# Layer 0's modulation vectors: from 128-column stationary blocks of w_mod to a 2-column stationary silu(c), with other planner settings

## The chip, the cores and the metric

The kernel runs on one core of a Trainium2 chip. The metric is the device time of one launch in microseconds (us). Before the change it is 2589.57 us, the median of three runs (2583.79, 2589.57 and 2592.41).

## The reference, cut to what matters

The reference is a two-layer backbone over 1024 latent tokens and 256 context tokens of width 1024, all in float32. Each layer normalises the tokens, scales and shifts them with modulation vectors, projects them by one large matrix, runs three branches (Fourier mixing F, differential attention A, a bidirectional state-space scan S), merges the branches by gates, and adds the result to the stream. The change touches the first lines of layer 0:

```
mod_l = jax.nn.silu(c) @ w_mod[l] + b_mod[l]          # (1, 1024) @ (1024, 3072)
mod_c = jax.nn.silu(c_ctx) @ w_mod[l] + b_mod[l]
sh_l, sc_l, g_l = jnp.split(mod_l[:, None, :], 3, axis=-1)
h_l = rmsnorm(x, norm_w[l]) * (1.0 + sc_l) + sh_l      # the same for the context with mod_c
... = jnp.split(h_l @ w_in[l], split_at, axis=-1)
```

Shift (part 0) and scale (part 1) for both vectors c and c_ctx are needed before anything can be projected. That is two products of a 2 x 1024 matrix with a 1024 x 1024 one, whose weights are 8 MB.

## The kernel before, in words

**Engines and planner.** TensorE (PE) does matrix products and transposes, VectorE (DVE) and ScalarE (ACT) the elementwise work, GpSimd (POOL) a few copies, and SyncE (SP) issues every transfer. The program is not in written order. Python generators ("threads") emit operations: `m` (the three branches), `p` (start and projections), `f` (normalisation of the later rows, merge, finish), `e` (gates of the last branch), `g` (layer 1's modulation and both gate vectors); weight loading and splitting is tagged `w`. While the program is built, a list scheduler (class Scheduler) keeps a modelled clock for each engine, and each time places the ready operation of the best priority. The priority is the number of the operation in order of emission less `BIAS[thread]`. A thread may have at most `AHEAD[thread]` emitted operations that are not yet placed. So the order on each engine is fixed at build time, and another cost or setting anywhere can redraw the order of the whole program. Nearly all instructions are issued by one line, L400 (`o.fn(...)`), so profile rows are told apart by their tiles.

**Storage.** There are 28 slots of 128 x 1288 floats (tile `ar`) for everything large, and eight PSUM banks (tile `ps`). A bank is given out when its first matmul is placed.

**Layer 0's start** (`start`, `mod0`). Ten slots are reserved for the tokens. `mod0` goes over k = 0..7 (row blocks of w_mod) and, in each, over part 1 and part 0: it loads one 128 x 1024 tile (512 KB), and for each of its eight 128-column blocks it issues one float32 matmul with the block stationary and `cs[:, k]` (128 x 2: silu of c and of c_ctx) moving. All 128 matmuls accumulate into one bank t (128 x 32), which a matmul with a zeroed operand clears. The result stands with channels on partitions, as the next step wants it. Between the tiles the loop issues other loads: the constants with k = 1, layer 0's parameters with k = 3, the first four token tiles with k = X_AT (4), and the first projection weight (`fu01`, two raw tiles) with k = W_AT (7). Then modT is formed from bank t, `mod_finish` makes the scale and shift `ab`, and `norm_T` transposes the normalised tokens and applies `ab`. The first projection (`proj_fu`) comes after that. The remaining six token tiles are loaded once `mod0` has been emitted.

**The rest.** All large products are float16 pairs (high and low part, three products each). In layer 1 the branches run in the order F, A, S. S goes through its chunks one after the other (`ssd_scan`), then come the last merge and the output.

Of the kernel before, what the change touches and what calls it, by code (L numbers as in the profile page):

```python
# [14 lines left out]
AF = mybir.ActivationFunctionType  # L15
# [28 lines left out]
NSLOT = 28  # L44
NW = 8
RAW = 2
BIAS = {'m': 1200, 'p': 300, 'w': 1000, 'f': 0, 'e': -50000, 'g': -100000}
AHEAD = {'m': 120, 'p': 120, 'f': 40, 'e': 27, 'g': 6}
MAXB = {'m': 4, 'p': 3, 'f': 3, 'e': 1, 'w': 1, 'g': 1}
LEAST = (1, 1)  # L50
WLIM = {'p': 2, 'f': 4, 'e': 1}
# [2 lines left out]
RES = 2  # L54
BOR, BMAX = 2, 4
HOLD = 0.25
X_AT, W_AT = 4, 7
G_AFTER = 'fu2'
F_START, F_FIN = 1000, 300
C_FIN = (2, 2)  # L60
# [90 lines left out]
class Scheduler:  # L151
# [3 lines left out]
    def __init__(self, nc):  # L155
# [11 lines left out]
        self.fixed = []  # L167
        self.bias = dict(BIAS)
        self.slot_of = {}
# [248 lines left out]
class Builder:  # L418
# [316 lines left out]
    def mod0(self, L):  # L735

        nc, V = self.nc, self.nc.vector
        t = self.mm(True)
        nc.bias['w'] = 0
        zero = self.small(32)  # L740
        nc.gpsimd.memset(zero, 0.0)
        for k in range(8):
            for part in (1, 0):
                yield ('slots', 1)
                s = self.alloc()
                nc.sync.dma_start(s.v(1024), self.A['wm'][0, part, k])
                if k == 0 and part:
                    self.mul(t[:, 0:32], s.v(1024)[:, 0:128], zero, True, False)
                for b in range(8):
                    c = 16 * part + 2 * b  # L750
                    self.mul(t[:, c:c + 2], s.v(1024)[:, b * 128:b * 128 + 128], self.cs[:, k], False, k == 7 and not part and b == 7)
                s.drop()
            if k == 1:
                self.consts()
            if k == 3:
                self.params(0)
            if k == X_AT:
                self.load_x(0)
            if k == W_AT:
                self.fetch_p = True  # L760
                self.prefetch()
        modT = self.cst.tile([128, 16, 2], F32, name="modT0")
        V.tensor_tensor(modT, t[:, :32].rearrange("p (b s) -> p b s", s=2), self.pv[0][:, 0:16].unsqueeze(2).to_broadcast([128, 16, 2]), ALU.add)
        nc.close('p', True)
        self.mod_finish(L, modT)
        nc.bias['w'] = BIAS['w']
        yield
# [107 lines left out]
    def start_rest(self, L):  # L875
        yield ('need', (0, 'h0'))
        self.nc.bias['f'] = F_START
        for i in (1, 2):
            self.norm_scale(self.groups[i], self.x[i])
            yield from self.norm_T(L, self.groups[i], self.x[i])  # L880
        self.nc.bias['f'] = BIAS['f']

# [797 lines left out]
    def finish(self, L, N):  # L1680
# [76 lines left out]
        if l == 0:  # L1757
            yield from steps
        self.ahead['f'] = AHEAD['f']
        self.ev.add((l + 1, 'fin'))  # L1760
# [144 lines left out]
    def build(self, layers=2):  # L1905
        self.setup()
        self.layers, self.later = layers, 0
        self.ahead = dict(AHEAD)
        Ls = []
# [179 lines left out]
```

## Time and profile before

| | |
|---|---|
| median of three runs | 2589.57 us |
| the profiled execution's own time | 2585.78 us |
| its span, first to last instruction | 2584.0 us |
| TensorE busy in the span | 2486.6 us (96%) |
| VectorE, ScalarE busy | 1821.3 us (70%), 1268.0 us (49%) |
| mean granted TensorE clock | 0.983 |
| all 16 DMA engines' share of the span | 34.5% |

A float32 matmul or transpose in the program is two MATMUL records in the trace, so that the 128 products of `mod0` are 256 records. A matmul's record is longer than the distance to the next one, since matmuls are pipelined: the rate is read from many records in a row. A group's "busy" counts overlapping records once.

### The profile page before, as it was taken

To read this page: it belongs to the slowest core of one execution; us is meant where nothing else is said; L and a number is where in the kernel's file an instruction comes from. 1 tells how busy PE (TensorE), PEld (TensorE's weight loads), DVE (VectorE), ACT (ScalarE), POOL (GpSimd) and SP (SyncE) were. 2 spreads that over 40 slices of the span, in tenths; PEclk is the share of its full clock that TensorE was granted. 3 is DMA by queue.
4 is the path that set the end of the run, shared out by engine and by line. 5 is a ranking of instruction groups with operands and counts; after the bars stand their busy time and mean duration, and the time that the engine had idled before them with its cause. 6 is when DMAs were issued, how large, how long until landed. Compare 5 with 4: busy or idle time off the path is not lost. (4 is left out here: it accounts for less than half of the span.)

```text
span 2584.0 us, 42400 instructions
## 1 busy us (share of the span) xinstructions
PE 2486.6 (96%) x16800; PEld 1572.5 (61%) x16800; DVE 1821.3 (70%) x3823; ACT 1268.0 (49%) x2398; POOL 47.5 (2%) x93
## 2 busy tenths in 40 slices
PE   9999999999999999999999999999999999998698
PEld 9655665657565665575587556555655556556467
DVE  1868565687877898468956775776477768748766
ACT  2654453545655564456513654554464656446221
POOL 0200000000000000000000000000000000000000
PEclk9999999999999999999999999999999999999699
DMA  6132243354433334213722122434343423232331
GB/s 250 50 131 77 65 101 82 80 148 111 112 78 89 131 116 142 87 55 119 286 79 99 57 90 66 109 94 98 82 122 88 100 95 106 78 102 87 131 131 66
DMA packets 256979, 270.61 MB, mean 105 GB/s; under 512 B 181062, under 2 KB 191110, under 8 KB 256780
## 3 DMA queue, kind: packets, MB, share of 16 engines
q1 hardware_dynamic: 256780, 267.89, 34.5%
q8 instruction: 132, 2.16, 0.3%
q14 instruction: 67, 0.55, 0.1%
HBM read 178.02 MB, written 36.88 MB: 83 GB/s over the span
## 5 line engine op out<-in xcount | busy, mean ns | idle before, releaser
L400 PE MATMUL ps<-ar,w 128*128 128x512 f16 (+1 forms) x7296 | 1476.8, 355 | 3.7 <-ACT w L400 2.7
L400 PEld LDWEIGHTS <-w 128*128 128x128 f16 x7296 | 708.7, 98 | 649.6 <-issue 17.0
L400 PEld LDWEIGHTS <-ar 128*128 128x128 f16 x8000 | 648.9, 98 | 231.3 <-issue 26.4
L400 PE MATMUL ps<-ar,ar 128*128 128x128 f16 (+4 forms) x4564 | 564.7, 274 | 31.2 <-DVE ar L400 18.4
L400 PE MATMUL ps<-w,ar 128*128 128x256 f16 x3312 | 396.0, 273 | 0.0
L400 ACT ACTIVATE ar<-ps,s1m,qksc 128x1280 f32<-128x1280 f32 (+1 forms) x144 | 190.1, 1320 | 194.4 <-DVE s1m L400 158.0
L400 DVE TENSOR_REDUCE s1m<-ps 128x1 f32<-128x1280 f32 (+1 forms) x144 | 196.9, 1368 | 101.8 <-PE ps L400 91.0
L400 ACT ACTIVATE w<-raw 128x1024 f16<-128x1024 f32 x147 | 154.5, 1051 | 180.9 <-PE ps L400 105.5
L400 ACT ACTIVATE ar<-ar 128x1280 f16<-128x1280 f32 (+5 forms) x140 | 138.1, 987 | 104.6 <-DVE ar L400 103.0
L400 DVE TENSOR_TENSOR ar<-ar,ar 128x1280 f16<-128x1280 f32 (+3 forms) x116 | 123.4, 1064 | 9.3 <-ACT ar L400 9.0
L400 DVE SCALAR_TENSOR_TENSOR ar<-ar,pv,ar 128x1284 f32<-128x1284 f32 (+1 forms) x64 | 97.1, 1517 | 32.9 <-ACT ar L400 32.3
L400 ACT ACTIVATE ar<-ps 128x128 f32<-128x128 f32 (+5 forms) x192 | 67.3, 386 | 104.6 <-PE ps L400 103.6
L400 ACT ACTIVATE ar<-ps,ds 128x512 f32<-128x512 f32 (+1 forms) x86 | 53.9, 627 | 114.4 <-PE ps L400 114.3
L400 DVE SCALAR_TENSOR_TENSOR ar<-ar,s1m,ar 128x1280 f32<-128x1280 f32 (+1 forms) x72 | 103.1, 1432 | 0.0
L400 ACT ACTIVATE ar<-ar,ar 128x128 f32<-128x128 f32 x288 | 90.1, 388 | 22.8 <-DMA ar<-rows 21.7
L400 ACT ACTIVATE w<-raw,s1p 128x1024 f16<-128x1024 f32 x72 | 79.0, 1138 | 33.9 <-DVE s1p L400 33.7
L400 DVE SCALAR_TENSOR_TENSOR w<-raw,s1p,w 128x1024 f16<-128x1024 f32 x72 | 89.8, 1279 | 7.9 <-ACT w L400 7.7
L400 PE MATMUL ps<-k,ar 128*128 128x128 f32 (+1 forms) x492 | 79.3, 289 | 15.5 <-DVE ar L400 14.7
L400 DVE SCALAR_TENSOR_TENSOR w<-raw,s1f,w 128x1024 f16<-128x1024 f32 x65 | 81.4, 1279 | 9.8 <-ACT w L400 9.8
L400 PEld LDWEIGHTS ps<-k,ar 128*128 128x128 f32 x492 | 63.1, 157 | 38.2 <-DVE ar L400 23.3
L400 DVE SCALAR_TENSOR_TENSOR scrf<-ps,ds,ar 128x256 f32<-128x256 f32 x72 | 34.7, 482 | 72.6 <-PE ps L400 72.3
L400 PEld LDWEIGHTS ps<-ar,ar 128*128 128x128 f32 x428 | 67.0, 206 | 29.7 <-DVE ar L400 20.8
(218 smaller groups left out, 2157.0 us busy)
## 6 DMA issues: line engine op xcount, KB each, us to landing
raw<-in_wt SPq DMA_DIRECT2D x160, 512.0 KB, 4.7
ar<-in_wm SPq DMA_DIRECT2D x48, 512.0 KB, 6.4
ar<-rows SPq DMA_DIRECT2D x36, 512.0 KB, 4.5
yp<-scrf SPq DMA_DIRECT2D x64, 256.0 KB, 2.2
ar<-in_x SPq DMA_DIRECT2D x20, 512.0 KB, 9.5
gs<-scre SPq DMA_DIRECT2D x32, 256.0 KB, 2.0
scrf<-yp SPq DMA_DIRECT2D x32, 256.0 KB, 2.7
ar<-ar SPq DMA_DIRECT2D x32, 160.0 KB, 2.8
```

What stands on the lines that cost most here:

```text
L400: o.fn(*(place(a) for a in o.args), **{k: place(a) for k, a in o.kw.items()})
```

## The change

`mod0` makes silu(c) the stationary operand (128 x 2) and streams the w_mod tile in two halves of 512 columns. Each part has two banks of 2 x 512, so that 32 matmuls replace the 128. The results stand with channels along the free dimension on two partitions. For each part ScalarE copies one half and VectorE the other into a row slot (two more slots), and 16 TensorE transposes of 2 x 128 bring the channels back onto partitions, into a bank t as before. The zeroed operand, its memset and its matmul are gone. Beside that, six planner settings change: the biases of m, p and w, the lookahead of m and f, and X_AT.

```diff
-BIAS = {'m': 1200, 'p': 300, 'w': 1000, 'f': 0, 'e': -50000, 'g': -100000}
-AHEAD = {'m': 120, 'p': 120, 'f': 40, 'e': 27, 'g': 6}
+BIAS = {'m': 1000, 'p': 200, 'w': 400, 'f': 0, 'e': -50000, 'g': -100000}
+AHEAD = {'m': 80, 'p': 120, 'f': 30, 'e': 27, 'g': 6}
-X_AT, W_AT = 4, 7
+X_AT, W_AT = 3, 7
     def mod0(self, L):
-        t = self.mm(True)
+        row = [self.alloc(), self.alloc()]
+        p = [[self.mm(True), self.mm(True)] for _ in range(2)]
         nc.bias['w'] = 0
-        zero = self.small(32)
-        nc.gpsimd.memset(zero, 0.0)
         for k in range(8):
             for part in (1, 0):
                 yield ('slots', 1)
                 s = self.alloc()
                 nc.sync.dma_start(s.v(1024), self.A['wm'][0, part, k])
-                if k == 0 and part:
-                    self.mul(t[:, 0:32], s.v(1024)[:, 0:128], zero, True, False)
-                for b in range(8):
-                    c = 16 * part + 2 * b
-                    self.mul(t[:, c:c + 2], s.v(1024)[:, b * 128:b * 128 + 128], self.cs[:, k], False, k == 7 and not part and b == 7)
+                for i in range(2):
+                    self.mul(p[part][i][:2], self.cs[:, k], s.v(1024)[:, i * 512:i * 512 + 512], k == 0, k == 7)
                 s.drop()
...
+        t = self.mm(True)
+        for part in (1, 0):
+            for i in range(2):
+                r = row[part].v(1024)[:2, i * 512:i * 512 + 512]
+                if i:
+                    V.tensor_copy(r, p[part][i][:2])
+                else:
+                    nc.scalar.activation(r, p[part][i][:2], AF.Copy)
+            for b in range(8):
+                nc.tensor.transpose(t[:, 16 * part + 2 * b:16 * part + 2 * b + 2], row[part].v(1024)[:2, b * 128:b * 128 + 128], self.ident[:2, :2])
         modT = self.cst.tile([128, 16, 2], F32, name="modT0")
...
+        for r in row:
+            r.drop()
```

## Rows read from the trace of the kernel before

**Rows 1.** The page: the span, TensorE's busy time, its 40 slices in tenths.

```profile
span 2584.0 us, 42400 instructions
PE 2486.6 (96%) x16800; PEld 1572.5 (61%) x16800; DVE 1821.3 (70%) x3823; ACT 1268.0 (49%) x2398; POOL 47.5 (2%) x93
...
PE   9999999999999999999999999999999999998698
```

**Rows 2.** Stretch, its us, busy of PE, PEld, DVE, ACT, POOL; clock, DMA share, GB/s.

```profile
100.00:2300.00 2200.00, 2154.56 (x14768) 1324.00 (x14766) 1582.29 (x3210) 1128.58 (x2120) 32.36 (x71) 1.00 0.35 102
...
2380.00:2460.00 80.00, 48.27 (x198) 31.64 (x196) 59.26 (x167) 29.13 (x71) 0.00 (x0) 0.68 0.35 121
```

**Rows 3.** Timeline of the start, 0 to 110 us: start, us, engine, operation, count, idle before.

```profile
5.04 0.60 PE L400 MATMUL ps<-s,ar 128*128 128x32 f32 x2 [5.04 <-DMA ar<-in_wm]
...
5.46 54.75 PE L400 MATMUL ps<-cs,ar 128*128 128x2 f32 x256
...
11.91 4.13 SPq L400 DMA_DIRECT2D ar<-in_x  x4
...
16.09 6.99 SPq L400 DMA_DIRECT2D ar<-in_wm  x6
...
34.19 1.06 ACT L400 ACTIVATE w<-raw 128x1024 f16<-128x1024 f32 x1 [7.70 <-DMA raw<-in_wt]
```

**Rows 4.** The same timeline around the end of mod0 (56 to 130 us).

```profile
60.25 0.19 DVE L400 TENSOR_TENSOR modT<-ps,pv 128x32 f32<-128x32 f32 x1 [23.45 <-PE ps L400]
...
68.40 7.33 PE L400 MATMUL ps<-k,ar 128*128 128x128 f32 x36 [2.74 <-DVE ar L400]
...
75.80 3.83 PE L400 MATMUL ps<-ar,w 128*128 128x512 f16 x17
```

**Rows 5.** Stretches of the start, as in Rows 2: what the transfers moved.

```profile
0.00:10.00 10.00, 4.96 (x24) 4.99 (x24) 0.35 (x2) 1.50 (x2) 0.33 (x5) 1.00 0.77 289
10.00:20.00 10.00, 10.00 (x49) 10.00 (x48) 0.42 (x2) 0.00 (x0) 0.00 (x0) 1.00 0.88 351
20.00:30.00 10.00, 10.00 (x49) 10.00 (x49) 3.10 (x13) 4.59 (x8) 0.00 (x0) 1.00 1.03 411
...
40.00:50.00 10.00, 10.00 (x48) 10.00 (x49) 0.00 (x0) 0.00 (x0) 0.00 (x0) 1.00 0.41 154
```

**Rows 6.** The tile in_wm, 0 to 70 us: issue to landing.

```profile
DMA to landing us min/median/max: 6.5/9.5/10.2
```

**Rows 7.** Stretches, as in Rows 2, in which TensorE does only 128x128 float32 transposes.

```profile
61.48:64.09 2.61, 2.61 (x13) 2.61 (x13) 2.21 (x10) 2.61 (x6) 0.12 (x1) 1.00 0.00 0
64.29:65.66 1.37, 1.37 (x13) 1.13 (x11) 1.20 (x7) 1.37 (x3) 0.82 (x2) 1.00 0.13 33
67.80:74.40 6.60, 5.88 (x26) 5.16 (x27) 6.09 (x8) 3.90 (x6) 3.17 (x4) 0.50 0.03 6
74.60:75.60 1.00, 1.00 (x11) 0.95 (x10) 1.00 (x2) 1.00 (x3) 1.00 (x2) 1.00 0.96 352
```

**Rows 8.** TensorE's timeline: a one-column stationary operand and 512 float32 columns moving.

```profile
957.27 1.02 PE L400 MATMUL ps<-ar,k 128*1 128x512 f32 x2
```

**Rows 9.** Groups by form: line engine operation shapes xcount, busy us, mean ns, idle before.

```profile
L400 PE MATMUL ps<-ar,k 128*1 128x512 f32 x12 | 6.0, 591 | 0.0
...
L400 ACT ACTIVATE ar<-ps 128x512 f32<-128x512 f32 x24 | 13.6, 591 | 23.5 <-PE ps L400 23.5
...
L400 DVE SCALAR_TENSOR_TENSOR ar<-ps,ar 128x512 f16<-128x512 f32 x20 | 13.2, 685 | 3.5 <-ACT ar L400 3.3
```

**Rows 10.** TensorE's timeline in layer 1's scan, two of its chunks, with the idle time before.

```profile
2417.70 1.19 PE L400 MATMUL ps<-scrm,ar 128*128 128x256 f32 x2 [2.96 <-ACT scrm L400]
...
2422.13 1.97 PE L400 MATMUL ps<-ar,ar 128*128 128x64 f32 x8 [2.80 <-DVE ar L400]
...
2433.30 1.97 PE L400 MATMUL ps<-ar,ar 128*128 128x64 f32 x8 [2.80 <-DVE ar L400]
```

**Rows 11.** Stretches, as in Rows 2, over the same scan in layer 0.

```profile
1100.00:1220.00 120.00, 114.56 (x744) 79.35 (x742) 93.61 (x229) 70.58 (x184) 0.00 (x0) 0.97 0.27 90
```

## The prediction

> **What bounds the kernel now.** I read the page first, then the busy times by stretch, then the timeline of the start and of the worst stretch. On the page TensorE is busy 2486.6 of 2584.0 us, and nearly every slice is at nine tenths [rows 1]. The stretches tell where the other 97 us are. From 100 to 2300 us only 45.4 us are idle in 2200 [rows 2], so through the long middle the kernel is as long as TensorE's work: a microsecond of TensorE time that goes before 100 us moves everything behind it forward. Two places are not dense. One is 2380 to 2460 us, with 31.7 us idle and a granted clock of 0.68 [rows 2], which is layer 1's scan. The other is the start, where TensorE looks busy but does little: from 5.46 us on, 256 records of two moving columns take 54.75 us, or 213.9 ns each [rows 3], and VectorE sits idle 23.45 us before it can form modT at 60.25 [rows 4]. The transfers aren't that late: they run at 411 GB/s from 20 to 30 us, and 154 GB/s from 40 to 50 is 3.7 us at that rate: they are done at about 44 [rows 5]. So the start is bound by TensorE's 54.75 us.
>
> One thing must be read with care. The clock column shows 1.00 up to 64 us, yet the transposes just behind `mod0` are 13 records in 2.61 us (201 ns), while the same ones from 64.29 on are 13 in 1.37 us (105 ns). Later ones at a granted 0.50 come 26 in 5.88 busy us (226 ns, with gaps), and at 1.00 it is 11 in 1.00 us (91 ns) [rows 7]. I conclude that the column has no entry before 64 us, and that TensorE stood at its lower level of 1.2 GHz through all of `mod0`: two moving columns at a time never raised it.
>
> **The change part by part.**
>
> *The wide products.* 32 products make 64 records with 512 moving columns. The nearest row has a stationary operand of one column and 512 float32 columns: two records in 1.02 us [rows 8], each 591 ns long [rows 9], so the second starts 1.02 - 0.59 = 0.43 us after the first. That is at 2.4 GHz; 64 x 0.427 = 27.3 us. At the lower level it would be twice that, 54.6 us.
>
> *The level at the start.* TensorE idles 5.04 us until the first tile lands [rows 3] and starts low. How soon do wide matmuls raise the level? After 61.48 us transposes of 128 columns did so by 64.29, some 2.8 us later; after 68.40 they were granted 1.00 by 74.60, 6.2 us later, with pauses between them [rows 4, 7]. Half of such a stretch is lost: 1.4 to 3.1 us. I take 3.0 us, since matmuls may also wait for tiles in it; the ends are 0 and 27.3 (it never rises, a rival below).
>
> *Waits for w_mod.* One tile is 524 KB, at 411 GB/s 1.28 us [rows 5], and gives TensorE 4 x 0.427 = 1.71 us of work. So TensorE is behind the transfers, not ahead of them. X_AT moves SP's four token transfers ahead of two w_mod tiles; the eight tiles loaded before them are 13.7 us of work plus 3.0, which reaches to about 21.7 us. The ninth tile lands near 21.7 too (7.1 MB end with it, and by 20 us 6.4 MB had moved: 2.9 and 3.5 in the first two stretches [rows 5]). I take 0.5 us of waiting; the ends are 0 and 5.1 (the four token tiles' 4 x 1.28). The last w_mod tile is issued by 23.1 us [rows 3] and lands at most 10.2 us later [rows 6], at 33.3. With its own work that is 35.0, not later than TensorE's 5.04 + 27.3 + 3.0 + 0.5 = 35.8 us. No queue is held: SP issues the same transfers, the tokens only earlier, and POOL loses one memset.
>
> *Copies and transposes.* Each copy moves 512 elements from PSUM: 591 ns on ScalarE, at most 685 ns on VectorE [rows 9], side by side, both engines idle then. Part 1's copies lie beside part 0's last tile, and part 0's beside part 1's transposes. The 16 transposes are 32 records, on the path. At the upper level 32 x 0.105 = 3.4 us, at the lower 32 x 0.201 = 6.4 [rows 7]. I take 3.5 us and 0.3 for two hand-overs (0 to 1.0, a copy and a bit, if the cover fails). modT is then at 39.6 us instead of 60.25: 20.6 us gained.
>
> *Behind it.* From modT to the first projection (75.80) are 15.5 us [rows 4], in which token transposes at the lower level wait for ScalarE's and VectorE's steps. Their 39 low records take 8.5 us, where 105 ns each would make 4.1 [rows 7]; the 4.4 us mostly hide behind the other engines, and the two-column transposes may let the level fall again. I take 1.0 us gained; the ends are 4.4 gained and, where the stage has to wait for transfers until 44, as much lost. Is anything late next? `fu01` has landed by 34.19 [rows 3], and its split can run before 39.6. The tokens of the later rows and the Fourier tables land by 44 and are wanted after the first projection has begun. So nothing is.
>
> *The settings.* The thresholds by which a starved operation overtakes shift by 100 to 600 operations, and m and f look less far ahead. No row shows what that is worth; it redraws the idle time of the whole order. At the best the scan in layer 1 is covered: 31.7 us of idle time, and about 15 us lost by the low level there (0.32 of 48.27 busy us) [rows 2]. At the worst more chunks of it stand uncovered. Chunks there start 11.17 us apart with 5.8 us of pauses each, and their matmuls run low [rows 10], say 8.9 us with the level. Four more of them are 36 us. Between -47 and +36 I take -4, near nothing, on the side of a better cover because layer 0's like stretch has just 5.4 us idle in 120 [rows 11].
>
> The sum on the profiled execution: 2585.8 (span 2584.0 and 1.8 around it) - 20.6 - 1.0 - 4 = 2560.2 us. That execution lies 3.8 us under the median of the runs shown, and within their 8.6 us, so a median may come out a few us higher; I forecast 2560.
>
> The Trainium skill (TensorE: Matmul & The Clock Gate, "HAM oscillation — how this bites in real kernels") speaks against the change: if a tile's matmuls are shorter than the wait for the next tile, the clock falls back on every tile. By it the wide products would stay low, which is the first rival. The trace bears on its condition: 1.71 us of work for a tile against 1.28 us of transfer, so it shouldn't hold here beyond the token gap.
>
> **The rivals.**
> 1. *The clock stays low in `mod0`.* For it: it was low there for 55 us [rows 3, 7]. Against it: two columns at a time are hardly work, and dense transposes raised it in some 3 us. Then the products take 54.6 us as before, and the transposes 6.4: modT at 5.0 + 54.6 + 6.7 = 66.3, 6 us later than now. 2585.8 + 6 - 4 = 2588: no change.
> 2. *The new order covers layer 1's scan.* For it: the worst idle stretch is there, and layer 0's is covered. Against it: TensorE's filling work simply ran out at 2380 us, and m loses bias. Half of the 47 us makes 2564.2 - 23.5 = 2541.
> 3. *The start gives part back.* `mod0` now ends while transfers still run (until 44 us), so weights, tokens of the later rows or TensorE's own low level hold the stage behind it: 4.4 us from 39.6 to 44, the 1.0 us not gained, and 2.6 us if the other 25 transposes run low too. 2560.2 + 8.0 = 2568.
> 4. *The other side.* m has less bias and looks less far ahead, so the fillers (projections, merge) are used up earlier and more of layer 1's scan stands alone at the end, at 8.9 us a chunk. 2564.2 + 4 x 8.9 = 2600: slower. It decides from the third chunk on (2591). For it: the fillers do run out there already. Against it: the biases keep their order, and m still precedes f by 1000 operations.
>
> **How the numbers follow.** Forecast 0.50 (2560, own range 2550 to 2572), rival 1 0.06, rival 2 0.22, rival 3 0.15, rival 4 0.07. 0.3% of 2589.57 is 7.8 us, about what a measurement can tell from no change: faster is under 2581.8, slower over 2597.3. Rivals 2 and 3 and the forecast are faster but for some 0.05 of their upper ends: 0.82. Rival 1 and those ends are 0.11 for the same, rival 4 is 0.07. The range 2541 to 2586 leaves out about half of rival 2 below, and rivals 4 and half of 1 above.
>
> **What would show it.** In the profile after: 64 records of 512 columns, 0.43 us apart but for the first few; modT near 39.6 us; the first projection near 54; the stretch from 100 to 2300 us as dense as now. The settings' term is read in the scan of layer 1: how much idle time lies in its 80 us, now 31.7. The forecast is wrong if the wide records stay 0.85 us apart, if the first projection comes after 62, or if idle time near the end grows by more than 20 us.

## The result, and the profile after

The changed kernel takes 2540.94 us (median of four runs, 2539.77 to 2543.32), the kernel before 2586.83 beside it: a ratio of 0.9821, 95% interval 0.9800 to 0.9842, or 45.9 us less. The forecast was 2560; the time lies 19 us below it, 0.06 us under the lower end of the range, and on the figure of rival 2 (2541). The four runs spread over 3.6 us, so the 0.06 us say nothing by themselves; the terms of the sum do. The profiled execution took 2540.84 us, 44.9 less than that of before.

The page of the changed kernel, the lines that answer to [rows 1]:

```profile
span 2539.0 us, 42040 instructions
...
PE 2459.8 (97%) x16622; PEld 1524.4 (60%) x16622; DVE 1814.8 (71%) x3825; ACT 1272.9 (50%) x2400; POOL 49.1 (2%) x92
...
PE   8999999999999999999999999999999999999998
```

TensorE is busy 26.8 us less (2486.6 to 2459.8) and idle 18.2 us less (97.4 to 79.2), which together is the span's 45.0. Busy time goes where a product becomes cheaper or its clock higher; idle time goes where an order gets better. The last four slices, 8, 6, 9, 8 in [rows 1], now read 9, 9, 9, 8.

The changed kernel's start, TensorE's timeline (start, us, engine, operation, shapes, count, idle before); it answers to [rows 3, 4]:

```profile
6.18 30.45 PE L400 MATMUL ps<-ar,cs 128*2 128x512 f32 x64 [6.18 <-DMA ar<-in_wm]
...
36.57 1.38 PE L400 MATMUL ps<-k,ar 2*128 2x2 f32 x16
...
53.70 2.75 PE L400 MATMUL ps<-ar,w 128*128 128x512 f16 x12
```

The 256 narrow records of 54.75 us have become 64 wide ones of 30.45. The first projection starts at 53.70 us instead of 75.80, 22.1 earlier. The same stretch, ScalarE's and VectorE's part:

```profile
34.10 0.59 ACT L400 ACTIVATE ar<-ps 2x512 f32<-2x512 f32 x1
...
34.96 0.68 DVE L400 COPY ar<-ps 2x512 f32<-2x512 f32 x1 [7.37 <-PE ps L400]
...
36.67 0.57 ACT L400 ACTIVATE ar<-ps 2x512 f32<-2x512 f32 x1
36.68 0.68 DVE L400 COPY ar<-ps 2x512 f32<-2x512 f32 x1 [0.75 <-PE ps L400]
...
37.98 0.19 DVE L400 TENSOR_TENSOR modT<-ps,pv 128x32 f32<-128x32 f32 x1 [0.63 <-PE ps L400]
```

modT is formed at 37.98 us, 22.3 us before its old time of 60.25 [rows 4]. How far apart the wide records are is read from their weight loads, one for each (the engine PEld of the same stretch):

```profile
10.40 0.13 PEld L400 LDWEIGHTS ps<-ar,cs 128*2 128x2 f32 x1 [0.73 <-issue]
11.26 0.13 PEld L400 LDWEIGHTS ps<-ar,cs 128*2 128x2 f32 x1 [0.73 <-issue]
12.01 0.09 PEld L400 LDWEIGHTS ps<-ar,cs 128*2 128x2 f32 x1 [0.63 <-issue]
12.44 0.09 PEld L400 LDWEIGHTS ps<-ar,cs 128*2 128x2 f32 x1 [0.34 <-issue]
...
22.68 0.15 PEld L400 LDWEIGHTS ps<-ar,cs 128*2 128x2 f32 x2 [0.71 <-DMA ar<-in_wm]
23.17 0.09 PEld L400 LDWEIGHTS ps<-ar,cs 128*2 128x2 f32 x1 [0.34 <-issue]
```

The first seven stand 0.85 us apart (TensorE at 1.2 GHz), those from 12.01 us on 0.43 (2.4 GHz), as the forecast had it. One load waits 0.71 us for a tile, at 22.68, but the products lose nothing by it: 7 x 0.85 + 57 x 0.43 us is all of their 30.45, and TensorE's own list of waits up to 60 us (us in all, times, longest) names w_mod once, for the first tile:

```profile
PE ps L400 <- DMA ar<-in_wm: 6.2, 1, 6.2
```

Now the far end. Busy time by stretch over layer 1's second scan, first the kernel before (stretch, its us, busy of PE, PEld, DVE, ACT, POOL; clock, DMA share, GB/s):

```profile
2300.00:2500.00 200.00, 167.45 (x909) 104.09 (x907) 151.19 (x347) 92.44 (x202) 0.00 (x0) 0.87 0.37 128
```

The changed kernel, its middle and the same scan, which answer to [rows 2]:

```profile
100.00:2250.00 2150.00, 2097.16 (x14372) 1296.87 (x14370) 1538.70 (x3123) 1092.73 (x2058) 34.13 (x71) 0.99 0.35 99
...
2340.00:2420.00 80.00, 78.95 (x403) 42.61 (x402) 73.48 (x193) 44.35 (x97) 0.00 (x0) 1.00 0.49 173
2300.00:2500.00 200.00, 197.06 (x1263) 129.53 (x1263) 159.62 (x395) 92.31 (x202) 0.00 (x0) 1.00 0.40 144
```

In these 200 us the idle time falls from 32.6 to 2.9 us, and the granted clock rises from 0.87 to 1.00. The middle got worse: 52.8 us idle in 2150 where it was 45.4 in 2200. TensorE's timeline in the scan shows what the new order put there; it answers to [rows 10]:

```profile
2363.96 1.10 PE L400 MATMUL ps<-ar,ar 128*128 128x64 f32 x8
...
2365.82 2.97 PE L400 MATMUL ps<-ar,w 128*128 128x512 f16 x13
2368.96 0.67 PE L400 MATMUL ps<-scrm,ar 128*128 128x256 f32 x2 [0.16 <-ACT scrm L400]
...
2369.68 4.05 PE L400 MATMUL ps<-ar,w 128*128 128x512 f16 x18
2373.57 1.00 PE L400 MATMUL ps<-ar,ar 128*128 128x64 f32 x8
```

Between the steps of a chunk now stand float16 products of 512 columns, the merge's: where TensorE waited 2.80 to 2.96 us it works. A chunk takes 9.6 us instead of 11.17, and its eight small products 1.00 to 1.10 us instead of 1.97, where the granted clock of the stretch is now 1.00.

### The profile page after: what moved, and what is told of

Read it like the earlier page. It is cut to its first block, busy times and chain, and to the rows that moved or that the text cites. A ratio compares the mean times of both kernels' runs of the same rounds, so it can differ in the third digit from the quotient of the medians.

```text
span 2539.0 us, 42040 instructions
## 1 busy us (share of the span) xinstructions
PE 2459.8 (97%) x16622; PEld 1524.4 (60%) x16622; DVE 1814.8 (71%) x3825; ACT 1272.9 (50%) x2400; POOL 49.1 (2%) x92
## 5 line engine op out<-in xcount | busy, mean ns | idle before, releaser
L400 PE MATMUL ps<-ar,w 128*128 128x512 f16 (+1 forms) x7296 | 1495.7, 356 | 6.1 <-ACT w L400 5.3
L400 PE MATMUL ps<-ar,ar 128*128 128x128 f16 (+3 forms) x4564 | 562.6, 273 | 17.1 <-ACT ar L400 5.1
L400 PE MATMUL ps<-w,ar 128*128 128x256 f16 x3312 | 412.1, 273 | 0.6 <-DVE H L400 0.4
L400 ACT ACTIVATE ar<-ps 128x128 f32<-128x128 f32 (+4 forms) x194 | 68.8, 386 | 118.7 <-PE ps L400 116.8
L400 PE MATMUL ps<-k,ar 128*128 128x128 f32 (+2 forms) x508 | 84.5, 294 | 17.1 <-DVE ar L400 14.2
L400 ACT ACTIVATE scrf<-ps,ds 128x512 f32<-128x512 f32 (+1 forms) x80 | 51.1, 639 | 84.0 <-PE ps L400 73.1
L400 PEld LDWEIGHTS ps<-k,ar 128*128 128x128 f32 (+1 forms) x508 | 67.1, 160 | 42.2 <-DVE ar L400 21.8
L400 DVE TENSOR_TENSOR ar<-ar 128x512 f32<-128x512 f32 (+4 forms) x142 | 77.0, 565 | 15.1 <-ACT ar L400 14.4
L400 DVE SCALAR_TENSOR_TENSOR w<-raw,s1f,w 128x1024 f16<-128x1024 f32 x63 | 79.2, 1279 | 8.0 <-ACT w L400 8.0
```

The lines of the kernel that those rows point to most:

```text
L400: o.fn(*(place(a) for a in o.args), **{k: place(a) for k, a in o.kw.items()})
```

## The experiments

They take the change apart in two ways: by its parts (E1 to E5), and by the mechanism that the parts pointed to (E6 to E13). Diffs are against the changed kernel unless the text says otherwise. Times of E1 to E4 stand beside 2584.47 us of the kernel before, E5 to E8 beside 2583.86, E9 to E12 beside 2584.72, E13 beside 2586.24.

**E1, new start, old settings.**

```diff
+BIAS = {'m': 1200, 'p': 300, 'w': 1000, ...}
+AHEAD = {'m': 120, 'p': 120, 'f': 40, ...}
+X_AT, W_AT = 4, 7
```

> The wide products of the change with all six settings of before (BIAS, AHEAD and X_AT 4). Before is 2586.8 us, the changed kernel 2540.9; modT came 22.3 us earlier, so 23.6 us of the gain are not the start's. Theory S (the settings earn them, by covering layer 1's second scan): this run keeps the start's 22 us alone, 2565 us, and its last scan shows 25 us or more of TensorE idle time in 80 us, as before (31.7). Theory M (the earlier start redraws the order, and the settings matter little): 2541 us, with under 8 us idle in that scan. Theory C (the order is redrawn by any edit, and neither part owns the cover): anything from 2541 to 2590; then the idle time in the scan follows the total.

Measured: 2673.70 us, ratio 1.0340 (1.0324 to 1.0355): 89 us slower than before, though modT is formed at 37.52 us. The stretch in which it is lost, of E1:

```profile
700.00:900.00 200.00, 137.25 (x1060) 84.11 (x1057) 153.72 (x255) 89.99 (x168) 0.82 (x12) 0.79 0.37 95
```

62.8 us are idle in 200, at a clock of 0.79; the same stretch of the kernel before is busy for 196.09. It lies in layer 0's attention heads. What is missing there is seen in the gate thread's writes (tile `gs`): E1 issues two from 500 to 900 us (at 512.3 and 518.2), the changed kernel 14 from 510.3 to 823.4.

**E2, old start, new settings** (the kernel before with the three new lines of settings).

> The kernel before with the six new settings, its two-column products kept. Theory S: 2587 - 23.6 = 2563 us, last scan covered (under 8 us idle). Theory M: 2587 us, scan bare. Theory C: anything from 2541 to 2610.

Measured: 2641.12 us, ratio 1.0216 (1.0199 to 1.0234), modT at 60.26 us. From 700 to 900 us TensorE is busy for 151.84 at a clock of 0.84: the same hole. So the settings aren't better in themselves.

**E3, the change with the old AHEAD, and E4, with the old BIAS.**

```diff
 E3: +AHEAD = {'m': 120, 'p': 120, 'f': 40, ...}
 E4: +BIAS = {'m': 1200, 'p': 300, 'w': 1000, ...}
```

> The changed kernel with AHEAD for m and f back at 120 and 40 (BIAS and X_AT new). If under theory S the shorter lookahead carries the cover: 2565 us with a bare scan; if BIAS carries it: 2541 with a covered one. Theory M: 2541.

> The changed kernel with BIAS for m, p and w back at 1200, 300 and 1000 (AHEAD and X_AT new). If under theory S BIAS carries the cover: 2565 us with a bare scan; if AHEAD carries it: 2541 with a covered one. Theory M: 2541.

Measured: E3 2671.98 us, ratio 1.0337 (1.0322 to 1.0353), with the hole again (138.66 us busy of 700 to 900). E4 2592.45 us, ratio 1.0030 (1.0021 to 1.0040), without that hole but with smaller ones in layer 1: of E4,

```profile
2000.00:2100.00 100.00, 80.30 (x527) 45.73 (x525) 70.92 (x111) 55.91 (x99) 0.68 (x10) 0.91 0.31 72
2400.00:2500.00 100.00, 86.63 (x442) 47.02 (x442) 69.61 (x167) 47.30 (x75) 0.00 (x0) 0.91 0.57 200
```

The settings can't be told apart one by one: each mixture is another order of the whole program, and all four mixtures are slower than either whole kernel. None of the theories had these times; all four lie above what was expected. But what theory S says of layer 1's second scan comes out in E2. The 85 us from 75 before the start of the scan's last product on tile `scrm` to 10 behind it, in the kernel before and in E2:

```profile
2353.87:2438.87 85.00, 56.74 (x266) 37.94 (x264) 61.62 (x161) 42.59 (x118) 0.00 (x0) 0.75 0.37 122
...
2377.69:2462.69 85.00, 82.32 (x450) 48.52 (x449) 76.13 (x198) 52.65 (x138) 0.00 (x0) 1.00 0.35 115
```

With the old start the new settings leave 2.7 us idle there instead of 28.3 (2.2 in the change, 1.4 in E3, 11.5 in E4, 18.3 in E1). They do cover the scan; what E2 and E3 lose, they lose in layer 0.

**E5, the new start alone, with the order of before behind it.** Old settings; within the start the planner is told durations with which modT comes at its old modelled time, so that the succession on every engine from modT on is that of the kernel before; for that the numbers of the operations and the order in which banks are given out are adjusted too. Both copies of a part run on VectorE.

```diff
+nc.plan = 2676.0 if k == 7 and not part and not i else 892.0
...
-if i: V.tensor_copy(...)  else: nc.scalar.activation(..., AF.Copy)
+V.tensor_copy(r, p[part][i][:2])
...
+nc.plan = nc.plag = 0.0
```

> The wide products with all settings of before, and the planner told durations for the start by which it draws the very order of before: from modT on, every engine's sequence of operations is that of before (only slot numbers differ, and both copies of a part are VectorE's). So this run has the new start alone. E1 had the same start and settings, another order, and 2673.7 us. Theory O (the order is worth what the start is not): before less the 22.3 us by which modT came earlier, 2584.5 - 22.3 = 2562 us (2556 to 2568), scan of layer 1 bare as before (about 32 us idle in 80). Rival (the wide start itself costs time later, and E1 shows it): over 2600 us.

Measured: 2560.92 us, ratio 0.9910 (0.9895 to 0.9925), 22.9 us less than before; modT at 37.36 us, 22.9 earlier. What the start gains arrives at the end undiminished. The scan is as bare as in the kernel before, with 32.4 us idle in the same 200 (32.6):

```profile
2300.00:2500.00 200.00, 167.63 (x1014) 114.50 (x1012) 146.40 (x352) 82.12 (x187) 0.00 (x0) 0.87 0.33 114
```

So the other 45.9 - 22.9 = 23.0 us of the change are the redrawn order's. That the copies are shared gains 0.15 to 0.3 us: from the end of the last product to modT it is 1.50 us with both on VectorE (E5) and 1.35 to 1.21 shared (the change, E9).

**How the order decides.** The program has eight half-tile buffers for split weights (NW = 8), two for a weight tile. `prefetch` hands a pair that comes free to the threads in the order p, f, e (p, e, f while the merge stands at certain steps). In the orders as they are written out, a pair comes free between 500 and 600 us of the planner's clock. In the kernel before and in the changed one the gate thread gets it, for `g21`; in E1 to E3 the merge thread holds two pairs for `oa0` and `g10`, products that can't start before the attention ends. The gate thread then has no weights, and the attention heads run with nothing beside them. E6 to E8 move such a handing-over by itself.

**E6, E1 with a hold** (against E1): the merge doesn't take `g10` of layer 0 before head 3 (`at3`) is done.

```diff
+if k == 'f' and (l, name) == (0, 'g10') and (0, 'at3') not in self.ev:
+    break
```

> E1's kernel with one line more in the planner: the merge's gate weight g10 of layer 0 is not loaded before layer 0's attention is done. In E1 the planner gives the last four free weight buffers to oa0 and g10, which wait for the end of attention, and the gate thread stops after its second block for lack of a buffer; TensorE then stands idle for 63 us from 700 to 900 us, beside bare attention heads. Theory G (the buffers decide whether filling work stands beside layer 0's attention): the hole closes to under 20 us of idle time in 700 to 900, gates are written there again, and the time falls by 60 to 90 us, to 2585 to 2615. Rival H (attention in E1 is slow for another reason, ScalarE or the transfers): 2655 to 2680, hole as wide.

Measured: 2624.83 us, ratio 1.0158 (1.0141 to 1.0175), 48.9 under E1, but above the range expected. Of E6:

```profile
700.00:900.00 200.00, 182.42 (x1427) 108.53 (x1425) 154.82 (x284) 114.51 (x212) 4.56 (x17) 0.95 0.41 102
...
900.00:1300.00 400.00, 358.19 (x2150) 233.00 (x2149) 272.61 (x617) 199.24 (x477) 0.51 (x10) 0.93 0.30 96
```

The hole closes (idle 62.8 to 17.6), and a part of it comes back later: from 900 to 1300 us 41.8 are idle, 12.2 in E1. By 900 us 20 gate writes have gone out since 500 (14 in the changed kernel), so less of the gate is left for layer 0's scans; that this is the whole of the loss wasn't tried. Layer 1's second scan is covered in this order too, with the old settings (2.8 us idle in the like 85), so the new settings are one way to that cover and not the only one.

**E7, the change with the gate's weights held**: `g21` isn't taken before head 3 is done.

```diff
+if k == 'e' and (l, name) == (0, 'g21') and (0, 'at3') not in self.ev:
+    break
```

> The changed kernel with the second gate weight of layer 0 (g21) held back until layer 0's attention is done: the opposite edit. Theory G: a hole of 30 to 60 us opens from 700 to 900 us as in E1 and E2, and the time rises by 55 to 90 us, to 2595 to 2630. Rival H: it stays within 10 us of 2541.

Measured: 2596.32 us, ratio 1.0050 (1.0035 to 1.0065), 55 us above the change. From 700 to 900 us it is busy for 155.56 at a clock of 0.84 (193.36 in the changed kernel), with two gate writes from 500 to 900. One hold of one weight tile takes the whole gain.

**E8, the kernel before with a hold in layer 1** (against the kernel before): the merge doesn't take `oa1` before the first scan group (`sc0`) is done, so that its products are left for the second.

```diff
+if k == 'f' and (l, name) == (1, 'oa1') and (1, 'sc0') not in self.ev:
+    break
```

> The kernel before with layer 1's merge weight oa1 held back until the first scan of layer 1 is done, so that merge products are left for the second scan. In that scan the kernel before has 37 records of 512-column float16 products, the changed kernel 165. Theory F (the exposed scan lacks filling work, and keeping some for it is what the new order did): idle time from 2380 to 2460 falls from 31.7 us to under 12, and the time by 12 to 25 us, to 2560 to 2573. Rival (the scan is bare because the branches came late, whatever the merge does): 2580 to 2590.

Measured: 2568.41 us, ratio 0.9941 (0.9926 to 0.9956), 15.5 us less, with the old start and the old settings. The same 200 us of E8:

```profile
2300.00:2500.00 200.00, 178.58 (x1060) 116.26 (x1058) 152.31 (x357) 90.88 (x199) 0.00 (x0) 0.91 0.38 132
```

11.1 us of idle time went, a third, and the clock rose from 0.87 to 0.91. 21.4 us of 2340 to 2440 are still idle. The time is in the range expected; the idle time from 2380 to 2460 is not: 17.7 us, where under 12 were expected.

**E9, the change with the tokens at their old place.**

```diff
-X_AT, W_AT = 3, 7
+X_AT, W_AT = 4, 7
```

> The change with one value of the kernel before: X_AT 4, so that the four token transfers go out behind the fifth pair of w_mod tiles again. Theory (the start's gain is the wide products', the rest is the cover of layer 1's second scan, and neither hangs on the tokens' place): modT comes 0.3 to 0.8 us earlier than in the changed kernel's 37.98, because the wait of 0.71 us for a tile at 22.68 goes, and the time is 2537 to 2543. Rival (a part of the 20 us behind the start comes from the tokens being there earlier): modT is the same or earlier, the first projection 1 to 5 us later, and the time above 2545. Rival (the token gap was worth more than its wait): below 2535.

Measured: 2533.88 us (2531.26 to 2537.61), ratio 0.9807 (0.9792 to 0.9823); modT at 37.13 us, 0.85 earlier. Both are a little beyond the theory's numbers, on the good side, and the time is in the range of the second rival (below 2535). Neither reason is shown. A weight load waits for a tile in this run too (0.61 us at 25.29), and modT is earlier because 4 records run 0.85 us apart and not 7. That number changes from run to run, also with the same start: it is 5 in E1 and 6 in E6, with modT at 37.52 and 38.02 us. At the first projection, 53.54 us and 53.70 in the change, little of it is left. So the token place shows no gain in the start, and the 7 us to the change (whose interval it overlaps) aren't explained by a row.

**E10, a threshold that the change doesn't touch.**

```diff
-AHEAD = {'m': 80, 'p': 120, ...}
+AHEAD = {'m': 80, 'p': 110, ...}
```

> The change with one value moved that the change itself leaves alone: AHEAD of the projections 110 instead of 120. Theory (what decides is which stage gets the pair of weight buffers that comes free near 500 us: with gate weights there are fillers beside layer 0's attention heads, with merge weights that can't be used yet there are none): written out, this order gives that pair to oa0 and g10 of the merge, so the same hole as with the old settings opens: TensorE busy under 170 us of the 200 from 700 to 900, fewer than 6 gate writes before 900, and a like hole in layer 1; the time is 2610 to 2670. Rival (the times of the changed settings E1 to E4 came from the particular values of the change, and ten operations less of look-ahead are small): 2541 to 2555.

Measured: 2633.40 us, ratio 1.0191 (1.0176 to 1.0207): 92 us above the change. Of E10:

```profile
700.00:900.00 200.00, 152.93 (x1070) 89.33 (x1070) 150.41 (x242) 88.38 (x160) 0.81 (x12) 0.80 0.35 95
```

The hole is there, with two gate writes from 500 to 900 us. The like hole in layer 1 is not: 1700 to 2100 us has 382.07 busy (388.41 in the change), 2100 to 2300 has 188.41 (196.72).

**E11, E10 with one rule more**: the merge doesn't take `oa0` before the gate has taken `g21`.

```diff
+if k == 'f' and (l, name) in ((0, 'oa0'), (1, 'oa0')) and self.wnext['e'] and self.wnext['e'][0] <= (l, 'g21'):
+    break
```

> The kernel of the experiment before (projections' look-ahead 110), with one rule more: the merge may not take a weight buffer for oa0 while the gate has not taken g21, in either layer. Nothing of the arithmetic and none of the thresholds changes. Theory (who gets the buffers near 500 us decides): most of the hole closes, TensorE busy 185 us or more of 700 to 900, over 10 gate writes before 900, and the time is 2545 to 2575, 60 us or more under the run without the rule. Rival (the look-ahead itself costs the time, by the projections being used up or late): within 20 us of the run without the rule.

Measured: 2540.15 us, ratio 0.9832 (0.9816 to 0.9849), 93 us under E10 and 5 better than expected. Of E11, with 14 gate writes from 641.3 to 832.0 us:

```profile
700.00:900.00 200.00, 189.16 (x1479) 123.98 (x1476) 167.92 (x305) 120.20 (x231) 1.20 (x12) 0.98 0.38 107
```

E10 and E11 have the same products, settings and start, and differ in one rule on who gets a pair of buffers, and in the order that follows from it. That shows the mechanism: 93 us hang on it, and ten operations of look-ahead by themselves cost nothing that shows.

**E12, the change with two values moved**: X_AT 4, and 35 for the merge's AHEAD.

```diff
+AHEAD = {'m': 80, 'p': 120, 'f': 35, ...}
+X_AT, W_AT = 4, 7
```

> The change with two values moved, meant as a version that beats it: X_AT 4 and AHEAD of the merge 35 instead of 30. The pairs of weight buffers go to the same stages in the same succession up to 2000 us as in the changed kernel. Theory: modT 0.3 to 0.8 us earlier by the token place, and a few microseconds from the merge looking further ahead in layer 0: 2531 to 2539. Rival (any move of a threshold costs, because these values stand in a narrow place): above 2548. Rival (nothing): 2539 to 2543.

Measured: 2530.10 us (2528.61 to 2533.57), ratio 0.9793 (0.9779 to 0.9808), just under the range expected; modT at 37.39 us, 0.59 earlier. All its runs lie below all of the change's (from 2539.77), but the kernel before beside them was 2.1 us faster too, and the two intervals overlap by a little. That it beats the change is likely, not shown.

**E13, E5 and E8 in one kernel.**

> E5 and E8 in one kernel: the new start with the order of the kernel before behind it, and oa1 of layer 1 held until that layer's first scan group is done. Theory (two terms that add: the start's, 2583.86 - 2560.92 = 22.9 us, and the cover of layer 1's second scan, 2583.86 - 2568.41 = 15.5 us): 22.9 + 15.5 = 38.4 us under the kernel before of the same call, about 2545, 2541 to 2550, so that of the change's 46 us some 7 are left for the rest of the new order. Rival (the two overlap, because the earlier start already frees filling work for that scan, or because the held weights are wanted sooner): at most 28 us under it, above 2556. Rival (the start gains more once the scan is covered): under 2538.

Measured: 2548.05 us, ratio 0.9841 (0.9818 to 0.9863), 38.2 us less than before where a sum of the two makes 38.4. The interval is 35 to 47 us less, so the rival of at most 28 is out: the start's gain and the scan's cover add up.

## Why the prediction was wrong, by its steps

*What bounds the kernel.* Right. As long as the order is kept, a microsecond at the start is worth one at the end: modT 22.9 us earlier in E5, and the kernel 22.9 us faster.

*The start, 20.6 us forecast, 22.3 measured.* Its parts: TensorE starts at 6.18 us and not at 5.04; both times it is the first tile that it waits for. 64 records, 0.427 us forecast apart and 0.43 measured. Low level at first, 3.0 forecast; seven records at 0.85 instead of 0.43 make 2.9 (that 3.0 came so close is luck: in the other runs with this start it is 4 to 7 records). Waits for later tiles, 0.5 forecast, none that TensorE felt. From the last product's end (36.63) to modT are 1.35 us, and 3.8 were forecast: the transposes are 16 records of 86 ns, not 32 of 105, and part 0's copies lie beside part 1's transposes, as forecast. The 32 came from the statement ahead that a float32 transpose is two records, which is wrong: the changed kernel's 426 float32 transposes of 128 x 128 are 426 records, and only its float32 products are two each. The rule of the Trainium skill that speaks against the change (TensorE: Matmul & The Clock Gate, "HAM oscillation — how this bites in real kernels") doesn't apply here: its condition isn't met, since the products wait for no tile but the first, and the records stay 0.43 us apart to the end. Rival 1 is out.

*Behind it, 1.0 us forecast, -0.2 measured.* From modT to the first projection it is 15.72 us, 15.55 before. The stage takes 0.2 us longer, where rival 3 had 7.0 (4.4 and 2.6); it is out too.

*The settings, -4 us forecast: the term that failed.* It measures 45.9 - 22.9 = -23.0 us, by the two intervals some 7 us more or less. Its sign and bounds (-47 to +36) held, its size is rival 2's: "The new order covers layer 1's scan", with -23.5 worked out for it. The mechanism is also rival 2's. E2 shows the cover with the settings alone, E8 gets 15.5 us by taking away a third of the scan's idle time in an otherwise old order, and E13 shows that this adds to the start. The other 23.0 - 15.5 = 7.5 us have no experiment of their own and aren't clear of the noise. They are a balance: in the changed kernel the lead shrinks from 22.3 us at modT to 8.6 at the first write of layer 0's result (1350.29 us, before 1358.86), and grows to 45 by the end. So that rival 2's number was met is in part luck: it took half of the 47 us by choice, while the new order takes nearly all of the scan's idle time (32.6 to 2.9 us) and pays a part of that back in layer 0.

The step's argument was wrong in its choice between far ends: "near nothing" was taken because no row showed what the settings are worth. But the rows did show where an order could still gain (31.7 us idle and the low level, [rows 2]), and the middle, with 45.4 us idle in 2200, had little left to gain and much to lose. E1 to E3 and E10 show that loss: 49 to 89 us more than the kernel before. With the start alone redrawing the order (E1) the time wasn't near 2560; it is reached where the order is kept by force (E5). Orders redrawn from the start on came out at 2530 to 2541 us (E9, E11, E12 and the change) or at 2592 and above (E1 to E4, E6, E7, E10), not between.

*Rival 4* named the right kind of danger at another place: the fillers ran out, in E1, not in layer 1's scan but beside layer 0's attention, because their weights had no buffer. (Its 8.9 us a chunk are also a little high: 5.8 us of pauses and half of the remaining 5.4 make 8.5.)

What stays open: why E9 and E12 are some us faster than the change, if they are (their first projections start at 53.54 and 53.79 us, the change's at 53.70, so it isn't the start), and which places the 7.5 us come from.

## What to carry to other kernels

When a list scheduler fixes the order of a whole program, a change has two prices: its own, which can be worked out from rows, and the redrawn order's, which is larger and comes in jumps; to know them apart, measure once with the old order kept. Look for what each stage needs in order to fill another's gaps (here a pair of weight buffers), and write that as a rule of the order, as E11 does, rather than hope that thresholds hit it. Float32 products with two columns moving are worth turning round: 256 records of 214 ns became 64 of 427.

## What the runs showed of the hardware

The spacing of like records tells TensorE's level where the page's clock column doesn't. The column reads 1.00 from 6 to 12 us of the changed kernel, while its records of 512 columns are 0.85 us apart there, and 0.43 behind:

```profile
6.00:12.00 6.00, 5.82 (x7) 0.88 (x8) 0.23 (x1) 0.00 (x0) 0.00 (x0) 1.00 1.02 411
```

Of the same transfers the old start made 54.75 us of narrow records one behind the other, at the lower level to their end: each of their 256 weight loads takes 333 ns, the first and the last alike, and the transposes behind them run at 201 ns where later ones take 105 [rows 7]. The wide ones stand at 2.4 GHz from 12.01 us on. So a TensorE that is busy in the profile without a pause isn't always one that has its clock. How many wide records run low first is not fixed: 4 in E5, E7 and E9, 7 in the change and E10. A transpose of a 2 x 128 block in float32 is one record of 86 ns (16 in 1.38 us).
